# The ConvFFN of a decoder step: the down-projection taken out of the token blocks and made a stage of its own in seven products

## The chip, the cores and the metric

The kernel runs on one core of one Trainium2 chip. The metric is the device time in microseconds of one execution, as the median of several runs. The engines are TensorE (PE in the rows, its weight loads PEld), VectorE (DVE), ScalarE (ACT), GpSimd (POOL) and SyncE (SP), whose queue issues the transfers between DRAM and the on-chip memory SBUF. Products accumulate in PSUM, which has eight banks of 512 float32 columns.

## The reference, cut to what matters

The whole program is one layer of a hybrid decoder for 2048 prompt tokens and 64 sample tokens (8 sequences of 8). The change is in its last part, the ConvFFN:

```python
hf = rmsnorm(x, w['norm_ffn'])
uf = hf @ w['f_wup']                                   # 1024 -> 2 x 2816
fa, fg = uf[..., :D_FF], uf[..., D_FF:]
f_ext = jnp.concatenate([f_buf.astype(fa.dtype), fa], axis=1)
fa_c = causal_dwconv(f_ext, w['f_conv_w'], w['f_conv_b'])   # 3 taps along the tokens
x = x + (jax.nn.gelu(fa_c) * fg) @ w['f_wdown']        # 2816 -> 1024
...
y = rmsnorm(x, norm_final)
```

The matrices are float32. Each factor is held as a high and a low part in `float32r`, and a product of a 128-row piece is three matmuls (`mm3`: high by high, high by low, low by high). Making the two parts of a tile is a "split": ACT casts the tile to its high part, and DVE or POOL subtracts that from the tile for the low part.

## The kernel before, in words

Everything before the ConvFFN (mLSTM, conv module, attention) is the same in both kernels. It leaves the tokens' rows in DRAM (`x2_d`). The ConvFFN then goes over four blocks of tokens, `C_BLOCKS`: three of 512 prompt tokens and one of 512 prompt tokens and the 64 sample tokens.

**Up-projection.** `block_input` reads a block's rows, normalises and transposes them, and writes seven sums of quarters `R[0]` to `R[6]` (for B11, B21, B22, T3, T1, T2, T4; the tokens are cut in two halves and the 1024 features in two halves). `load_pair` does the same on the weight side for two neighbouring tiles of 128 hidden features: it loads 1 MB of `f_wup`, adds and subtracts its quarters (`left_sums`, in the first block only; the later blocks read the sums back from DRAM, `sum_d`) and splits the seven factors into tiles `wt`. `seven_products` then makes two 128-feature tiles for both token halves with seven products in place of eight: each is 4 pieces by 3 matmuls, 12 matmuls with a half block's tokens as columns (256, and 288 in the last block). DVE joins the products from PSUM (`u`, `fe`). Two hidden tiles take one pair for `fa` and one for `fg`, that is 2 x 84 matmuls; between them the taps and the GELU are run (`y`), and after them `y` is multiplied by the second pair's results and split into `ht`.

**Down-projection.** After a group of 4 hidden tiles (`UP_GROUPS`; one group has 2), `load_down` loads and splits their `f_wdown` rows and multiplies `ht` by them: for each tile of 128 tokens and each half of the 1024 output columns, 3 matmuls of 512 columns per hidden tile. The results are added from PSUM to the residual rows `yt`. In program order a group's down-projection stands between the two pairs of the next group (`pend_down`), and the one of the last group of a block stands around `block_input` of the next block. After the last group the rows are normalised with `norm_final` and stored.

**Order.** The order in which each engine's instructions stand is made by a scheduler when the program is built, from data dependences and from the tiles that are free; each engine then runs its own list in order and waits on semaphores. All transfers are in SP's list; a transfer that waits for a tile to come free holds up those behind it. R has one buffer for each of its seven tiles, so the next block's `R[q]` can be written only when the last product that reads the old one is done. The raw weight tiles (`raw`, 4 KB a partition) have six buffers (`RAW_BUFS`), the split ones twelve.

Of the kernel before, what the change touches and what calls it, by code (L numbers as in the profile page):

```python
# [9 lines left out]
F32 = mybir.dt.float32  # L10
# [64 lines left out]
WT_BUFS = (7, 5)  # L75
XT_BUFS = 3
# [4 lines left out]
DOWN_SET = 4  # L81
U_BUFS = 6
UP_GROUPS = [4, 4, 4, 4, 2, 4]

C_BLOCKS = [(0, 0), (4, 0), (8, 0), (12, 1)]
BT = 4
HC = BT * P // 2
HS = S // 2
LO_POOL = (3, 5), (3, 5)
RAW_BUFS = 6  # L90
E_SUM = lambda nc: [nc.vector] * 4
MUL_POOL = (0, 1)


@with_exitstack
def trunk_kernel(ctx: ExitStack, tc: tile.TileContext, i: dict, o: list):
# [1341 lines left out]
    def rows_in(blk, own=(), junk=None):  # L1438

        t0, smp = blk  # L1440
        halves = []
        for z in range(2):
            xts = []
            for tid, r0, nt in [(t0 + 2 * z, 0, P), (t0 + 2 * z + 1, 0, P)] + ([(NT, z * HS, HS)] if smp else []):
                if nt < P or z in own:
                    t = fe_.tile([P, D], F32, name="xt", tag="xt", bufs=XT_BUFS)
                else:
                    t = xw.tile([P, D], F32, name="xt", tag="xt")
# [202 lines left out]
    ahead = rows_in(C_BLOCKS[0], (), junk_rows)  # L1651
# [3 lines left out]
    fe_ = ctx.enter_context(tc.tile_pool(name="fe", bufs=1, reuse_waits="tile"))  # L1655
    wtps = [ctx.enter_context(tc.tile_pool(name="wtf0", bufs=WT_BUFS[0], side="right", reuse_waits="tile"))]
    f2 = ctx.enter_context(tc.tile_pool(name="f2", bufs=2, side="right", reuse_waits="tile"))

    def utile(n):
        return fe_.tile([P, HC + HS], F32, name="u", tag="u", bufs=U_BUFS)[:, :n]  # L1660

    def block_input(blk, rows=None):

        t0, smp = blk
        n = HC + (HS if smp else 0)
        R = [fe_.tile([P, 2, KT // 2, HC + HS], F32R, name=f"R{q}", tag=f"R{q}") for q in range(7)]

# [8 lines left out]
        xts, xts1 = rows or rows_in(blk, (1,))  # L1676
        b11 = [fe_.tile([P, HC + HS], F32, name="b", tag="b", bufs=KT // 2)[:, :n] for _ in range(KT // 2)]

# [33 lines left out]
    def sample_state():  # L1712
        fsr = i["state_ffn_conv"][0].rearrange("b j c -> (b j) c")
        for q0 in range(0, FT, 8):
            nq = min(8, FT - q0)
            t = fe_.tile([P, D], F32, name="xt", tag="xt", bufs=XT_BUFS)
# [50 lines left out]
    def conv_states(q0, nq):  # L1767

        for src, dst, nr in ((carry, fconv_p[0, 0], 2), (cy_s, fconv_s[0].rearrange("b j c -> (b j) c"), 2 * NB)):
# [3 lines left out]
            t = f2.tile([P, BT * P + S], F32, name="fo", tag="y")  # L1773
# [6 lines left out]
    def parts(smp):  # L1780
        return ((slice(0, HC), 0), (slice(HC, HC + HS), 1)) if smp else ((slice(0, HC), 0),)

    for bi, (t0, smp) in enumerate(C_BLOCKS):
        R, n = nxt_.pop()
        npr = BT * P
        ntok = npr + (S if smp else 0)
        tiles = [(t0 + j, P) for j in range(BT)] + ([(NT, S)] if smp else [])
        ys = []
        for tid, nt in tiles:
            yt = xw.tile([P, D], F32, name="yt", tag="xt")  # L1790
            SY.dma_start(yt[:nt], x2_d[tid])
            ys.append(yt)
        if smp:
            sample_state()
        pend_down = []

        def load_down(fbase, gsz, hts, last_):

            wds = []
            for f0 in range(fbase, fbase + gsz, 2):  # L1800
                for z in range(2):
                    raw = raw_tile()
# [131 lines left out]
```

## Time and profile before

| | |
|---|---|
| time, median of 3 runs | 2969.03 us (2966.44 to 2973.68) |
| the profiled execution | 2968.27 us, span 2966.6 us |
| PE busy over the span | 2807.9 us (95%), 17924 matmuls |
| DVE, ACT, POOL busy | 2142.2 us (72%), 1534.5 us (52%), 1109.8 us (37%) |
| moved by DMA | 471.80 MB, 159 GB/s on average |
| ConvFFN | from 1452 us to the end at 2966.6 us |

Busy time is the union of an engine's instructions. A matmul's own duration in the rows is longer than its share of the stream, because matmuls follow each other in a pipeline; what one costs is read from the distance between starts. The chain of work that ended last is 72% PE and 14% DVE over the span.

### The profile page before, as it was taken

To read this page: it belongs to the slowest core of one execution; us is meant where nothing else is said; L and a number is where in the kernel's file an instruction comes from. 1 tells how busy PE (TensorE), PEld (TensorE's weight loads), DVE (VectorE), ACT (ScalarE), POOL (GpSimd) and SP (SyncE) were. 2 spreads that over 40 slices of the span, in tenths; PEclk is the share of its full clock that TensorE was granted. 3 is DMA by queue.
4 is the path that set the end of the run, shared out by engine and by line. 5 is a ranking of instruction groups with operands and counts; after the bars stand their busy time and mean duration, and the time that the engine had idled before them with its cause. 6 is when DMAs were issued, how large, how long until landed. Compare 5 with 4: busy or idle time off the path is not lost.

```text
span 2966.6 us, 49315 instructions
## 1 busy us (share of the span) xinstructions
PE 2807.9 (95%) x17924; PEld 2479.4 (84%) x17924; DVE 2142.2 (72%) x3937; ACT 1534.5 (52%) x3134; POOL 1109.8 (37%) x1299
## 2 busy tenths in 40 slices
PE   7999989999799799899899999999999999999998
PEld 6889889976678688676588988999989999899987
DVE  4588898873123888744598889878797767877776
ACT  4667678871232765412464446655466545544433
POOL 1558565451120632633433325333253222522222
PEclk9999999997899999999899999999999999999999
DMA  7644433244456423656745555655465545644432
GB/s 185 194 139 160 124 97 117 90 161 152 165 184 222 141 82 109 212 193 240 266 162 169 166 171 195 189 160 160 144 219 160 158 135 162 187 131 133 131 116 76
DMA packets 336939, 471.80 MB, mean 159 GB/s; under 512 B 33421, under 2 KB 238707, under 8 KB 336688
## 3 DMA queue, kind: packets, MB, share of 16 engines
q1 hardware_dynamic: 336696, 468.66, 49.2%
q8 instruction: 141, 2.31, 0.3%
q14 instruction: 102, 0.84, 0.1%
HBM read 361.68 MB, written 107.26 MB: 158 GB/s over the span
## 4 chain that ended last, share of the span: by engine, by line
PE 72%; DVE 14%; DMA 6%; issue 4%; ACT 2%; POOL 1%; SPq 1%; DVEq 0%; POOLq 0%; ACTq 0%
PE psA L150 21%; PE psD L150 14%; PE psF L150 14%; PE psE L150 9%; PE psG L150 9%; DVE psG L124 2%; DMA raw<-in_f_wup 2%; DVE wt L127 2%; PE psC L147 1%; PE psB L147 1%; DVE raw L127 1%; DVE acc L124 1%; DVE u L127 1%; DVE wf L127 1%; DMA xt<-x 1%
## 5 line engine op out<-in xcount | busy, mean ns | idle before, releaser
L296 ACT CAST wt<-raw 128x512 fp32r<-128x512 f32 x872 | 528.8, 620 | 529.2 <-PE psA L150 150.6
L127 DVE TENSOR_TENSOR wt<-raw,wt 128x512 fp32r<-128x512 f32 x660 | 512.2, 792 | 123.5 <-ACT wt L296 119.7
L127 POOL TENSOR_TENSOR wt<-raw,wt 128x512 fp32r<-128x512 f32 x212 | 306.5, 1449 | 703.9 <-ACT wt L296 572.2
L150 PE MATMUL psA<-R,wt 128*128 128x256 f32 (+1 forms) x2448 | 334.1, 287 | 4.1 <-DVE R L124 1.6
L150 PEld LDWEIGHTS psA<-R,wt 128*128 128x128 f32 x2448 | 313.8, 190 | 7.7 <-DVE R L124 1.8
L127 POOL TENSOR_TENSOR cside<-cside,cprod 128x512 f32<-128x512 f32 (+2 forms) x248 | 250.9, 1012 | 123.1 <-ACT cprod L119 90.0
L124 DVE SCALAR_TENSOR_TENSOR psG<-ue,vc,psG 128x512 f32<-128x512 f32 (+2 forms) x448 | 256.9, 573 | 22.8 <-ACT psG L119 16.0
L150 PE MATMUL psA<-wt,ht 128*128 128x512 f32 (+1 forms) x768 | 191.0, 395 | 0.0
L150 PE MATMUL psD<-R,wt 128*128 128x256 f32 (+1 forms) x1248 | 178.5, 288 | 6.7 <-DVE R L127 2.8
L150 PE MATMUL psF<-R,wt 128*128 128x256 f32 (+1 forms) x1248 | 179.3, 288 | 4.4 <-DVE R L124 1.7
L150 PE MATMUL psE<-R,wt 128*128 128x256 f32 (+1 forms) x1224 | 174.3, 287 | 5.8 <-DVE R L127 3.0
L150 PE MATMUL psG<-R,wt 128*128 128x256 f32 (+1 forms) x1224 | 175.3, 288 | 1.9 <-DVE R L124 1.3
L150 PEld LDWEIGHTS psD<-R,wt 128*128 128x128 f32 x1248 | 163.7, 191 | 10.4 <-DVE R L127 3.8
L150 PEld LDWEIGHTS psA<-wt,ht 128*128 128x128 f32 (+1 forms) x768 | 140.6, 185 | 34.9 <-DVE u L127 0.2
L150 PEld LDWEIGHTS psF<-R,wt 128*128 128x128 f32 x1248 | 163.4, 190 | 6.2 <-DVE u L127 2.6
L150 PEld LDWEIGHTS psE<-R,wt 128*128 128x128 f32 x1224 | 159.4, 190 | 9.6 <-DVE R L127 4.3
L150 PEld LDWEIGHTS psG<-R,wt 128*128 128x128 f32 x1224 | 160.3, 191 | 3.1 <-DVE R L124 1.6
L119 ACT ACTIVATE cprod<-ue,vc 128x512 f32<-128x512 f32 (+2 forms) x248 | 146.8, 605 | 28.4 <-POOL cside L127 22.0
L150 PE MATMUL psA<-wf,l 128*128 128x512 f32 x516 | 132.2, 404 | 10.8 <-DVE u L127 5.8
L124 DVE SCALAR_TENSOR_TENSOR y<-fe,vc,y 128x512 f32<-128x512 f32 x176 | 130.5, 778 | 14.4 <-ACT y L119 14.4
L127 POOL TENSOR_TENSOR y<-y,u 128x256 f32<-128x256 f32 x110 | 97.8, 898 | 107.0 <-DVE u L127 89.5
L150 PEld LDWEIGHTS psA<-wf,l 128*128 128x128 f32 x516 | 97.8, 193 | 38.7 <-issue 13.2
(608 smaller groups left out, 6096.1 us busy)
## 6 DMA issues: line engine op xcount, KB each, us to landing
raw<-sum SPq DMA_DIRECT2D x132, 512.0 KB
raw<-in_f_wup SPq DMA_DIRECT2D x110, 512.0 KB
raw<-in_f_wdown SPq DMA_DIRECT2D x88, 512.0 KB
xt<-x SPq DMA_DIRECT2D x48, 512.0 KB
sum<-raw SPq DMA_DIRECT2D x44, 512.0 KB
raw<-in_f_wup SPq DMA_DIRECT2D x66, 256.0 KB
xt<-in_x_prompt SPq DMA_DIRECT2D x32, 512.0 KB
x<-xt SPq DMA_DIRECT2D x32, 512.0 KB
```

Of the source, the lines that this page charges most:

```text
L119: A.activation(out, in_, func, bias=bias, scale=scale)
L124: V.scalar_tensor_tensor(out=out, in0=in0, scalar=s, in1=in1, op0=op0, op1=op1)
L127: (eng or V).tensor_tensor(out=out, in0=a, in1=b, op=op)
L147: T.transpose(out, in_, ident[:n, :n])
L150: T.matmul(out, lhsT, rhs, start=start, stop=stop)
L296: A.copy(hi, src)
```

## The change

The down-projection leaves the token blocks. The up-projection is run first for all tokens, in three blocks of 768, 640 and 640 prompt tokens (the last with the 64 sample tokens), so that a matmul has 384, 320 and 352 columns. For each pair of hidden tiles the gated product `y` is not split but summed: its quarters (token half by hidden tile) are combined by `left_sums` into the seven left factors of a product of the same kind, and these go to DRAM (`l_d`; the sample tokens' `y` to `ys_d`). Then a new stage makes the down-projection of the 2048 prompt tokens with seven products in place of eight, factor by factor: for each factor q, `right_factor` loads, adds and splits the eleven 128-row pieces of `f_wdown`'s quarter sums (`w`, 15 buffers), and for each of eight token groups j `left_factor` reads 128 token columns of all eleven pieces from `l_d` (`lr`, 2 buffers) and splits them (`l`, 3 buffers); 33 matmuls of 512 columns follow, and DVE or POOL adds the result to the residual rows `acc`, which stay in SBUF. The sample tokens are multiplied as before, with 132 matmuls. Two of the seven right factors are also written to DRAM and read again (`t2_d`, `t3_d`).

The raw tiles have 4 buffers instead of 6 in the up-projection, the split weights 10 instead of 12, and one of the four sums of the first block goes to POOL.

```diff
-WT_BUFS = (7, 5)
+WT_BUFS = (7, 3)
-UP_GROUPS = [4, 4, 4, 4, 2, 4]
-C_BLOCKS = [(0, 0), (4, 0), (8, 0), (12, 1)]
+C_BLOCKS = [(0, 6, 0), (6, 5, 0), (11, 5, 1)]
-RAW_BUFS = 6
-E_SUM = lambda nc: [nc.vector] * 4
+RAW_BUFS = 4
+E_SUM = lambda nc: [nc.vector, nc.vector, nc.gpsimd, nc.vector]
+DW_BUFS = 15
+E_LEFT = lambda nc: [nc.gpsimd, nc.vector, nc.vector, nc.gpsimd]
...
-                for y in yts:
-                    ht = f3.tile([P, 2, BT * P + S], F32R, name="ht", tag="ht")
-                    split(ht[:, 0, :ntok], ht[:, 1, :ntok], y[:, :ntok])
+            ls = f2.tile([P, 4, HM], F32, name="ls", tag="ls", bufs=1)[:, :, :hc]
+            (a11, a21), (a12, a22) = [[y[:, z, :hc] for z in range(2)] for y in ys]
+            left_sums(ls[:, 2], ls[:, 3], ls[:, 1], ls[:, 0], a11, a12, a21, a22, E_LEFT(nc))
+            SY.dma_start(l_d[bi][0, :, p], a11)
+            SY.dma_start(l_d[bi][1, :, p], a12)
+            SY.dma_start(l_d[bi][6, :, p], a22)
+            SY.dma_start(l_d[bi][2:6, :, p].rearrange("q p t -> p q t"), ls)
...
+            if bi + 1 < len(C_BLOCKS):
+                if p == FP - 3:
+                    rows_next = rows_in(C_BLOCKS[bi + 1])
+                if p == FP - 1:
+                    nxt_.append(block_input(C_BLOCKS[bi + 1], rows_next))
...
+    def right_factor(q, k):
...
+        elif q == T2:
+            t3, b, x = quarter(1, 1, k), quarter(0, 1, k), quarter(0, 0, k)
+            tt(t3, t3, b, ALU.subtract)
+            SY.dma_start(t3_d[k], t3)
+            tt(x, x, t3, ALU.add)
+            SY.dma_start(t2_d[k], x)
+        elif q == T3:
+            x = raw_w(t3_d[k])
...
+        w = dp.tile([P, 2, 512], F32R, name="w", tag="w", bufs=DW_BUFS)
+        split(w[:, 0], w[:, 1], x)
+        return w
+    def left_factor(q, j):
+        raw = dp.tile([P, FP, P], F32, name="lr", tag="lr", bufs=2)
+        r = 0
+        for b, c, m in segments(j):
+            SY.dma_start(raw[:, :, r:r + m], l_d[b][q, :, :, c:c + m])
+            r += m
+        w = dp.tile([P, 2, FP, P], F32R, name="l", tag="l", bufs=3)
+        split(w[:, 0], w[:, 1], raw)
+        return w
...
+    for qi, q in enumerate((B11, B21, T2, T3, T1, B22, T4)):
+        ws = [right_factor(q, k) for k in range(FP)]
...
+        for j in range(NJ):
+            l = left_factor(q, j)
+            if qi == 0 and j == 0:
+                accs = [[acc_rows(z, j) for j in range(NJ)] for z in range(2)]
+            pt = dps()
+            for k in range(FP):
+                mm3(pt, (l[:, 0, k], l[:, 1, k]), (ws[k][:, 0], ws[k][:, 1]), k == 0, k == FP - 1)
...
+            elif q == B22:
+                tt(x01, x01, pt, ALU.add)
+                out_rows_norm(0, j)
             else:
-                pend_down.append(down)
+                tt(x10, x10, pt, ALU.add)
+                out_rows_norm(1, j)
```

Three places show what the order of instructions becomes. The first is PE's list where one token block ends and the next begins (`R` with the larger number is the next block's, `wt,ht` is the down-projection, L147 the transposes of the next block's rows). Before, at the end of the second block:

```order
L150 MATMUL psF<-R_19466,wt 128x256 x12
L150 MATMUL psE<-R_19467,wt 128x256 x12
L150 MATMUL psA<-wt,ht 128x512 x6
L147 MATMUL psB<-ident,xt 128x128 x2
L147 MATMUL psC<-ident,xt 128x128 x2
L150 MATMUL psF<-wt,ht 128x512 x6
L150 MATMUL psG<-wt,ht 128x512 x6
```

And now, at the end of the first block, on the same engine (`R_18897` to `R_18899` are the next block's first three factors):

```order
L150 MATMUL psG<-R_15306,wt 128x384 x12
L150 MATMUL psD<-R_15307,wt 128x384 x12
L147 MATMUL psB<-ident,xt 128x128 x2
L147 MATMUL psB<-ident,xt 128x64
L147 MATMUL psC<-ident,xt 128x128 x2
L147 MATMUL psC<-ident,xt 128x64
L150 MATMUL psF<-R_18897,wt 128x320 x12
L150 MATMUL psE<-R_18898,wt 128x320 x7
L147 MATMUL psB<-ident,xt 128x64
L147 MATMUL psB<-ident,xt 128x128 x2
L150 MATMUL psE<-R_18898,wt 128x320 x3
```

Before, 96 matmuls of the last group's down-projection stand among the transposes; now only the next block's own products stand there.

The second place is SP's list at the end of the last block. Before, in the last block, weight loads of both projections alternate (L1744, L1749 and L1759 load `f_wup` pieces and their sums, L1775 stores the conv state, L1803 loads `f_wdown`):

```order
L1744 DMA raw<-in_f_wup 128x8x128
L1749 DMA raw<-in_f_wup 128x4x128
L1759 DMA raw<-sum_0_19275 128x1024
L1759 DMA raw<-sum_1_19276 128x1024
L1803 DMA raw<-in_f_wdown 128x1024 x4
```

Now the stage's first loads stand behind the last store of left factors (L1860; L1919 loads `f_wdown` pieces, L1958 left factors, L1911 residual rows):

```order
L1858 DMA l_15489<-y 128x320
L1863 DMA ys<-y 128x2x32
L1860 DMA l_15489<-ls 128x4x320
L1919 DMA raw<-in_f_wdown 128x512 x6
L1958 DMA lr<-l_15487 128x11x128
L1919 DMA raw<-in_f_wdown 128x512
L1911 DMA acc<-x_11_197 64x1024
L1919 DMA raw<-in_f_wdown 128x512 x2
L1911 DMA acc<-x_12_198 64x1024
```

Fifteen more loads of residual rows (L1911) or `f_wdown` pieces follow before the second left factor's load.

The third place is SP's list at the third product of the new stage, T2, which has no counterpart before (L1939 and L1941 store the two factors `t3` and `t2`, here of pieces 0 to 2):

```order
L1958 DMA lr<-l_15487 128x11x128 x3
L1958 DMA lr<-l_15488 128x11x128 x2
L1919 DMA raw<-in_f_wdown 128x512 x7
L1939 DMA t_0_26187<-raw 128x512
L1919 DMA raw<-in_f_wdown 128x512
L1941 DMA t_0_26176<-raw 128x512
L1939 DMA t_1_26188<-raw 128x512
L1919 DMA raw<-in_f_wdown 128x512 x2
L1941 DMA t_1_26177<-raw 128x512
```

Three loads and two stores of 256 KB alternate for each of the eleven pieces, with the loads of T2's first five left factors ahead of them; the `raw` tiles here (2 KB a partition) have six buffers. On PE the first three token groups of T2 stand interleaved, piece by piece.

## Rows read from the trace of the kernel before

**Rows 1.** Busy time by stretch: us, PE, PEld, DVE, ACT, POOL, PEclk, DMA share, GB/s.

```profile
1520.00:1840.00 320.00, 311.19 (x2088) 283.12 (x2087) 278.59 (x492) 156.01 (x281) 99.53 (x108) 1.00 0.49 159
1840.00:2190.00 350.00, 347.42 (x2414) 322.48 (x2413) 283.10 (x486) 192.62 (x344) 123.56 (x136) 1.00 0.54 169
```

**Rows 2.** PE's timeline in the second block: start us, us, what.

```profile
1912.77 2.92 PE L150 MATMUL psD<-wt,ht 128*128 128x512 f32 x12
1915.53 2.94 PE L150 MATMUL psF<-wt,ht 128*128 128x512 f32 x12
1918.31 1.59 PE L150 MATMUL psE<-R,wt 128*128 128x256 f32 x12
1919.74 3.02 PE L150 MATMUL psA<-R,wt 128*128 128x256 f32 x24
```

**Rows 3.** PE's timeline in the last block, 288 columns.

```profile
2733.62 3.36 PE L150 MATMUL psA<-R,wt 128*128 128x288 f32 x24
2736.82 0.70 PE L150 MATMUL psE<-R,wt 128*128 128x288 f32 x4
```

**Rows 4.** ACT's timeline: the first tap of the first, second and third block.

```profile
1495.63 1.51 ACT L119 ACTIVATE y<-fe,vc 128x512 f32<-128x512 f32 x2
...
1859.23 1.52 ACT L119 ACTIVATE y<-fe,vc 128x512 f32<-128x512 f32 x2
...
2209.24 1.52 ACT L119 ACTIVATE y<-fe,vc 128x512 f32<-128x512 f32 x2
```

**Rows 5.** DVE's groups by form in the ConvFFN: xcount | busy, mean ns.

```profile
L127 DVE TENSOR_TENSOR wt<-raw,wt 128x512 fp32r<-128x512 f32 x616 | 478.4, 794 | 62.4 <-ACT wt L296 58.9
L124 DVE SCALAR_TENSOR_TENSOR y<-fe,vc,y 128x512 f32<-128x512 f32 x176 | 130.5, 778 | 14.4 <-ACT y L119 14.4
L127 DVE TENSOR_TENSOR raw<-raw 128x512 f32<-128x512 f32 x88 | 64.7, 755 | 13.6 <-DMA raw<-in_f_wup 13.5
L127 DVE TENSOR_TENSOR u<-u,psA 128x256 f32<-128x256 f32 x110 | 44.6, 414 | 3.6 <-PE psA L150 1.9 <-ACT u L1067 0.6
L127 DVE TENSOR_TENSOR y<-y,u 128x256 f32<-128x256 f32 x88 | 38.5, 462 | 0.0
L127 DVE TENSOR_TENSOR u<-u,psA 128x288 f32<-128x288 f32 x38 | 16.7, 450 | 1.9 <-PE psA L150 1.4
L124 DVE SCALAR_TENSOR_TENSOR y<-fs,vc,y 128x64 f32<-128x64 f32 x44 | 15.0, 378 | 0.0
```

**Rows 6.** POOL's and ACT's groups by form in the ConvFFN.

```profile
L127 POOL TENSOR_TENSOR wt<-raw,wt 128x512 fp32r<-128x512 f32 x176 | 257.2, 1464 | 613.6 <-ACT wt L296 496.4 <-issue 52.8 <-DVE fe L127 40.1
L127 POOL TENSOR_TENSOR y<-y,u 128x256 f32<-128x256 f32 x88 | 85.1, 968 | 107.0 <-DVE u L127 89.5 <-ACT y L119 15.9 <-DVE y L124 1.3
L296 ACT CAST wt<-raw 128x512 fp32r<-128x512 f32 x792 | 480.7, 620 | 456.6 <-PE psA L150 149.8 <-PE psD L150 91.0 <-PE psE L150 77.3
```

**Rows 7.** Tile `raw`, second block: duration ns min/median/max, first and last start.

```profile
L127 DVE TENSOR_TENSOR wt<-raw,wt x149: 675/691/1671, 1849.8 to 2188.2; 128x512 fp32r<-128x512 f32 x149
```

**Rows 8.** Tile `R`, 1800 to 1890 us: the second block's factors being written.

```profile
L127 DVE TENSOR_TENSOR R<-u,R x12: 409/637/1175, 1824.0 to 1856.1; 128x256 fp32r<-128x256 f32 x12
L124 DVE SCALAR_TENSOR_TENSOR R<-psC,vc,R x6: 469/476/484, 1814.4 to 1849.0; 128x256 fp32r<-128x256 f32 x6
```

**Rows 9.** Busy time at the start of the ConvFFN, columns as in Rows 1.

```profile
1457.00:1462.00 5.00, 3.06 (x16) 2.66 (x16) 4.66 (x7) 3.93 (x9) 2.96 (x2) 0.80 1.11 338
1462.00:1467.00 5.00, 3.50 (x15) 2.72 (x15) 4.25 (x6) 1.66 (x4) 1.95 (x2) 0.54 1.02 414
1467.00:1472.00 5.00, 2.79 (x8) 1.94 (x9) 5.00 (x9) 4.14 (x9) 3.71 (x4) 0.50 1.03 398
1472.00:1477.00 5.00, 3.19 (x15) 2.77 (x14) 4.86 (x8) 1.91 (x6) 3.58 (x3) 0.50 0.86 268
```

**Rows 10.** PE's timeline at the same place; in brackets the idle time before.

```profile
1452.39 0.69 PE L147 MATMUL psB<-ident,xt 128*128 128x128 f32 x2 [4.08 <-ACT b L119]
...
1455.07 2.93 PE L150 MATMUL psA<-R,wt 128*128 128x256 f32 x12 [0.22 <-ACT R L119]
```

More of the change, by code (lines that the diff above doesn't have):

```diff
@@ L74 @@
 LOW = -3e38
-WT_BUFS = (7, 5)
-XT_BUFS = 3
+WT_BUFS = (7, 3)
 E_B = lambda nc: nc.vector
@@ L1436, in out_rows, with pieces, rows_in @@
             SY.dma_start(x2_d[t], xt)
-    def rows_in(blk, own=(), junk=None):
-        t0, smp = blk
+    def pieces(blk, z):
+        t0, nt, smp = blk
+        hc = nt * P // 2
+        r, end, out = t0 * P + z * hc, t0 * P + (z + 1) * hc, []
+        while r < end:
+            m = min(end, (r // P + 1) * P) - r
+            out.append((r // P, r % P, m))
+            r += m
+        return out + ([(NT, z * HS, HS)] if smp else [])
+    def rows_in(blk, junk=None):
         halves = []
@@ L1443, in rows_in @@
             xts = []
[L1444 to L1448, printed above, removed]
+            for tid, r0, nt in pieces(blk, z):
+                t = xw.tile([P, D], F32, name="xt", tag="xt")
                 SY.dma_start(t[:nt], x2_d[tid][r0:r0 + nt])
@@ L1650, in trunk_kernel @@
             pass
-    ahead = rows_in(C_BLOCKS[0], (), junk_rows)
+    ahead = rows_in(C_BLOCKS[0], junk_rows)
     aps.close()
@@ L1674, in feature @@
             return pt[:, :n]
-        xts, xts1 = rows or rows_in(blk, (1,))
-        b11 = [fe_.tile([P, HC + HS], F32, name="b", tag="b", bufs=KT // 2)[:, :n] for _ in range(KT // 2)]
+        xts, xts1 = rows
+        b11 = [fe_.tile([P, HM], F32, name="b", tag="b", bufs=KT // 2)[:, :n] for _ in range(KT // 2)]
         def put(q, k, x, eng=None, gain=None):
@@ L1778, in trunk_kernel @@
     wdn = i["f_wdown"][0]
-    def parts(smp):
-        return ((slice(0, HC), 0), (slice(HC, HC + HS), 1)) if smp else ((slice(0, HC), 0),)
-    for bi, (t0, smp) in enumerate(C_BLOCKS):
+    l_d = [dram(f"l{b}", [7, P, FP, nt * P // 2]) for b, (_, nt, _) in enumerate(C_BLOCKS)]
+    ys_d = dram("ys", [P, FT, S])
+    for bi, (t0, nt_, smp) in enumerate(C_BLOCKS):
         R, n = nxt_.pop()
[L1785 to L1792, printed above, removed]
+        hc = nt_ * P // 2
+        npr = nt_ * P
@@ new lines, in trunk_kernel, with segments @@
+    us.close()
+    dp = ctx.enter_context(tc.tile_pool(name="dp", bufs=1, reuse_waits="tile"))
+    dps = banks("A", "B", "C", "A", "D", "E", "F", "G")
+    NJ = L // 2 // P
+    starts = [0]
+    for _, nt_, _ in C_BLOCKS:
+        starts.append(starts[-1] + nt_ * P // 2)
+    def segments(j):
+        out, c = [], j * P
+        while c < (j + 1) * P:
+            b = max(b for b in range(len(C_BLOCKS)) if starts[b] <= c)
+            m = min((j + 1) * P, starts[b + 1]) - c
+            out.append((b, c - starts[b], m))
+            c += m
+        return out
@@ new lines, in token_rows, with acc_rows @@
+    def token_rows(z, j):
+        out, r = [], 0
+        for b, c, m in segments(j):
+            t0, nt_, _ = C_BLOCKS[b]
+            out.append((t0 * P + z * (nt_ * P // 2) + c, m, r))
+            r += m
+        return out
+    def acc_rows(z, j):
+        if z == 0 and j < 6:
+            t = xw.tile([P, D], F32, name="acc", tag="xt")
+        else:
+            t = dp.tile([P, D], F32, name="acc", tag=f"acc{z}_{j}")
+        for t0, m, r in token_rows(z, j):
+            while m:
+                k = min(m, P - t0 % P)
+                SY.dma_start(t[r:r + k], x2_d[t0 // P][t0 % P:t0 % P + k])
+                t0, m, r = t0 + k, m - k, r + k
+        return t
```

261 lines of the change are left out of this document (148 added, 113 removed).

## The prediction

> **What bounds the kernel now.** I read the busy time by stretch first. In the ConvFFN PE is busy in 347 of 350 us of the second block, DVE in 283 (81%); in the first block PE is at 97% and DVE at 87% [rows 1]. So I read PE's timeline for what one matmul costs in the stream, as the distance between starts: at 512 columns (1918.31 - 1912.77) / 24 = 231 ns, at 256 columns (1919.74 - 1918.31) / 12 = 119 ns [rows 2], at 288 columns (2736.82 - 2733.62) / 24 = 133 ns [rows 3]. The three lie on a line of 0.437 ns a column with some 7 ns a matmul on top; I read 175 ns at 384, 147 at 320 and 161 at 352 from it.
>
> A block of 512 tokens has 22 x 84 matmuls at 119 ns and 528 at 231 ns, 341 us, and 32 transposes, some 4 us. ACT's first tap stands 363.6 us after the one before it in the first block and 350.0 us in the second [rows 4]. The second block thus loses about 5 us, all that its change of block costs; the first loses 13.6 us more, and it is the one whose DVE also makes weight sums. PE's stream is the bound, and DVE at some 87% begins to hold it up. What the change takes from PE counts fully, and so does every place where it leaves PE without work.
>
> **The matmuls.** The up-projection's three blocks have the same columns in all, in 5544 matmuls instead of 7392: before 5544 x 119.2 + 1848 x 133.3 ns = 907 us, after 1848 x (175 + 147 + 161) = 893: -14 us. The down-projection of the prompt tokens goes from 2112 to 1848 matmuls of 512 columns: 264 x 231 ns = -61 us. The 132 for the sample tokens stay. Together **-75 us**. The Trainium skill ("TensorE: Matmul & The Clock Gate", section "Back-to-back issue gap") puts an isolated matmul at its columns over 2.4 GHz plus 2.5 ns. By that the sum here would be 1848 x 2.5 + 264 x 216 ns = -62 us; the rows stand above it at every width, so they decide.
>
> **The change of block, now uncovered.** Before, 96 matmuls of down-projection (22 us) stand on PE while DVE, ACT and POOL write the next `R`. Now PE has only the next block's own products. From the last product on, DVE's list has to reach the last `R`: four times two operations of 0.48, one of 0.48, three lower halves of 0.4 to 0.7 and a sum of some 0.6 us [rows 8], 3.9 us each at 256 columns and 4.4 at 320 by the slope of the joins [rows 5], so 18 us; among them stand the last pair's products and sums and two weight splits, 5 us. PE has 84 matmuls and 24 transposes for these 23 us, 15 us. It loses 9 us with the last matmuls, twice, against 5 us three times before: **+3 us**. Below, nothing is lost at all (-15). Above, the writing takes as long as now, 1814 to 1857 us [rows 8], 42 us less 15, twice: +39. I take the sum, since nothing else is queued on DVE there.
>
> **The start.** The first block has six tiles to normalise and R is half as wide again (DVE 17 to 23 us), but the two pairs that PE has beside it are longer by 2 x 84 x 56 ns = 9 us. I take nothing.
>
> **Inside the up-projection.** PE now needs 168 matmuls for two hidden tiles with no down-projection between. DVE needs, by busy time over count [rows 5], in the first block 10 splits at 0.78, 6 sums at 0.74, 14 joins at 0.54, 2 products at 0.58, 4 taps at 1.05 and 2 left sums at 0.58, 26.4 us of PE's 29.4 (90%); in the second 20.0 of 24.7 (81%); in the third, with small pieces for the sample tokens, 24.6 of 27.1 (91%). Two blocks stand where one stood at 87%. If each loses what that one lost, **+14 us** net. Below: none loses (-14); above stands the rival on the shared port.
>
> **Between the stages.** The new stage's first load stands behind the last store of left sums on SP. From the last product U, DVE has about six operations of 0.5 us and POOL one of 1.3 us: first load at U+5. Ahead of the first left factor's end lie its store (0.66 MB), six raw pieces (1.57 MB) and itself (0.72 MB); at 340 GB/s, a little under the mean of the four stretches of [rows 9], in which the DMA was full or nearly so, that is 9 us; its split of 1408 columns, 2.75 times the 512 one on ACT and DVE [rows 6, 7], takes 3.6. PE stands still from U to U+18. An idle time of 4 us now leaves the clock at half, and 12 matmuls take 2.93 us instead of 1.43 [rows 9, 10]; one product of 33 at half speed throughout would add 7.6 us, I take 3. The first product ends at U+28.6. Then the second left factor is late: ahead of it are 5.2 MB of residual rows and 1.3 MB of raw pieces, with itself 7.3 MB, 21 us behind the first, and a split: U+39, another 10 us. In all **+31 us**; at 414 GB/s, the best of the four stretches, 26; at 268, the worst, 39.
>
> **T2.** Each of its eleven pieces is three loads and two stores of 256 KB; of six raw tiles three hold a piece, and a load waits for the store before it. They cannot begin before B12's pieces leave the raw tiles, some 5 us after the last product E of B21. 14.4 MB at 340 GB/s is 42 us; with a split and the last matmuls T2's first three groups are done at E+52. PE has the sample parts (66 matmuls, 15 us) and three products (23 us), interleaved piece by piece, to E+38: **+14 us** (6 at 414, 25 at 268 GB/s). T1 and T4 load two pieces each ahead: **+2** (0 to 6). The other factors load one piece of 256 KB in 7.6 us / 11 of PE's time each, and DVE has about 5 of every 7.6 us to do there: nothing.
>
> **The sum:** -75 + 3 + 14 + 31 + 14 + 2 = -11 us. The profiled execution takes 2968.3 us, 0.8 below the median of the runs shown, so I forecast **2958 us**.
>
> **The rivals.**
> - *The forecast*, each wait near my value: 2938 to 2978 us, chance 0.42.
> - *The waits are hidden.* For it: the interleaved order of T2, and that a group's DVE work was hidden under PE in the second block. Against: nothing of PE's is left at the three places. With the lower bounds, -75 - 15 - 14 + 26 + 6 = -72, 2896; half the way to my sum is 2927. Range 2900 to 2938, chance 0.26.
> - *DVE and POOL shut each other out in the up-projection; slower.* DVE's split takes 691 ns at the median and 1671 at most [rows 7], mean 794 [rows 5]: it waits for something that is not in its own list. If DVE operations with both inputs in SBUF and POOL operations exclude each other, two hidden tiles of the first block need 17.2 us of DVE (splits, sums, taps, products) and 14.3 of POOL (four splits and two sums at 1.46, four products and sums at some 1.4 [rows 6]), 31.5 us against PE's 29.4; now it is 20.5 + 7.8 = 28.3 in the 33 us that a pair of tiles takes. If that can be filled wholly, the first block loses 23 us; if only to today's 86%, all three lose 145. The middle, 84, in place of my 28 gives 3014, the range 2978 to 3060. It decides from 20 us above my term. Against: the second block today is at 74% by this count and loses nothing, which says nothing on 90%. Chance 0.17. The Trainium skill has such a rule ("SBUF — State Buffer", section "Who interferes with whom"): a DVE instruction with two SBUF inputs contends with a GpSimd instruction that reads SBUF, and the later one fully blocks. The spread of the splits agrees with it.
> - *The DMA is slower than 340 GB/s in the new stage*: left factors come in rows of 512 bytes, stores and loads alternate. At 268 GB/s the last three terms are 39 + 25 + 6 in place of 47: 2981; lower still, or with PE's clock down longer, up to 3010. Chance 0.13.
> - A change that does not do what it says is excluded by the order: the matmuls are gone. 0.02 is left for the rest.
>
> **How the numbers follow.** About 0.3%, 9 us, is what a measurement can tell from no change. Of the forecast's 0.42, 0.22 lies below 2960, 0.17 within 0.3% and 0.03 above. Faster: 0.22 + 0.26 and half of the rest, 0.49; same 0.17; slower 0.03 + 0.17 + 0.13 and the rest, 0.34. The range 2908 to 3010 leaves out the end of the hidden case and most of the upper half of the port's, together under 0.2.
>
> **What would show it.** In the profile after: PE's starts 175, 147 and 161 ns apart in the three blocks; the first taps of the blocks some 350 us, then 285 apart; two changes of block with about 9 us of lost PE time; PE idle for some 18 us between the last `R` product and the first `w` product, with a load as releaser and the clock at half behind it, and idle again for 10 us before the second; DVE above 85% in the first and third block; T2's first 99 matmuls in some 37 us instead of 23. The prediction is wrong if PE's share in the up-projection falls under 95% (the port), if the gap between the stages is above 45 us or below 20, or if the third product is as dense as the others.

## The result, and the profile after

The changed kernel takes **3001.3 us** (2998.8 to 3003.7, four runs) against 2968.8 for the kernel before in the same session: ratio 1.0113, 95% interval 1.0098 to 1.0129. It is 1.1% slower. I forecast 2958 and faster at 0.49; the time lies in the range (2908 to 3010), on the other side of no change.

The page's first lines for the changed kernel, which answer to the table of before: PE's busy time falls by 40 us with 2096 matmuls and transposes less, and its share of the span falls from 95% to 92%.

```profile
span 2997.0 us, 44306 instructions
PE 2767.7 (92%) x15828; PEld 2436.1 (81%) x15828; DVE 2058.6 (69%) x3432; ACT 1407.6 (47%) x2795; POOL 1165.5 (39%) x1269
```

ACT's timeline, first and last tap of each of the three blocks (answers to [rows 4]):

```profile
1505.43 1.02 ACT L119 ACTIVATE y<-fe,vc 128x768 f32<-128x768 f32 x1
1822.33 1.95 ACT L119 ACTIVATE y<-fe,vc 128x768 f32<-128x768 f32 x2
1873.65 0.92 ACT L119 ACTIVATE y<-fe,vc 128x640 f32<-128x640 f32 x1
2121.09 1.74 ACT L119 ACTIVATE y<-fe,vc 128x640 f32<-128x640 f32 x2
2185.87 0.93 ACT L119 ACTIVATE y<-fe,vc 128x640 f32<-128x640 f32 x1 [0.54 <-DVE fe L127]
2457.80 1.74 ACT L119 ACTIVATE y<-fe,vc 128x640 f32<-128x640 f32 x2 [5.21 <-DVE fe L127]
```

A block's ten inner pairs of hidden tiles lie between its first and last tap, a change of block between the last tap of one and the first of the next. Busy time of these stretches and of three in the new stage, columns as in [rows 1]:

```profile
1505.40:1822.30 316.90, 295.96 (x1664) 290.20 (x1663) 284.60 (x377) 124.06 (x201) 157.82 (x139) 0.99 0.53 176
1822.30:1873.70 51.40, 45.11 (x209) 37.48 (x208) 42.01 (x69) 38.32 (x74) 30.91 (x37) 0.77 0.45 140
1873.70:2121.10 247.40, 247.40 (x1688) 247.17 (x1688) 214.48 (x323) 120.09 (x204) 115.57 (x121) 1.00 0.62 198
2121.10:2185.90 64.80, 57.20 (x245) 45.95 (x245) 43.21 (x74) 31.88 (x62) 30.07 (x33) 0.63 0.43 129
2185.90:2457.80 271.90, 271.53 (x1705) 270.07 (x1704) 245.19 (x451) 132.18 (x237) 136.97 (x160) 1.00 0.57 175
2470.00:2488.10 18.10, 0.68 (x7) 0.27 (x4) 7.76 (x16) 5.13 (x8) 3.21 (x3) 0.64 0.76 226
2488.10:2524.20 36.10, 20.09 (x67) 14.98 (x68) 11.55 (x13) 8.74 (x12) 0.00 (x0) 0.71 1.08 298
2651.70:2700.90 49.20, 32.68 (x104) 21.53 (x102) 26.11 (x37) 10.99 (x16) 4.07 (x3) 0.85 0.90 293
```

The second and third block run dense. Time goes in the first block, in both changes of block, before and behind the stage's first product (sixth and seventh row), and in T2 (last row). PE's timeline gives the price of a matmul at 384, 320, 352 and 512 columns, and the idle time ahead of the places where it stands (in brackets): the start, the second change (two rows), and the first two products of the stage.

```profile
1459.29 0.90 PE L147 MATMUL psB<-ident,xt 128*128 128x128 f32 x3 [14.62 <-ACT b L119]
...
1804.06 2.24 PE L150 MATMUL psG<-R,wt 128*128 128x384 f32 x12
1806.14 2.24 PE L150 MATMUL psA<-R,wt 128*128 128x384 f32 x12
...
1900.04 1.92 PE L150 MATMUL psG<-R,wt 128*128 128x320 f32 x12
1901.81 1.33 PE L150 MATMUL psF<-R,wt 128*128 128x320 f32 x8
...
2134.72 1.22 PE L147 MATMUL psB<-ident,xt 128*128 128x128 f32 x4 [2.63 <-ACT b L119]
2150.62 0.47 PE L147 MATMUL psB<-ident,xt 128*128 128x128 f32 x1 [4.03 <-ACT xt L119]
...
2301.88 2.08 PE L150 MATMUL psF<-R,wt 128*128 128x352 f32 x12
2303.80 2.08 PE L150 MATMUL psE<-R,wt 128*128 128x352 f32 x12
...
2488.10 1.22 PE L150 MATMUL psA<-w,l 128*128 128x512 f32 x2 [17.43 <-ACT l L296]
2513.28 1.22 PE L150 MATMUL psB<-w,l 128*128 128x512 f32 x2 [15.13 <-ACT l L296]
2524.19 7.64 PE L150 MATMUL psC<-w,l 128*128 128x512 f32 x33
2531.67 7.64 PE L150 MATMUL psA<-w,l 128*128 128x512 f32 x33
```

A matmul costs 2.08 / 12 = 173 ns at 384 columns, 1.77 / 12 = 147 at 320, 1.92 / 12 = 160 at 352 and 7.48 / 33 = 227 at 512. In the following table a stretch's loss is its length less its matmuls at these prices (before: at those of the prediction, 342.1 us for a block). Before, the third change of block has to be read too, which I had not done: the first tap of the last block in ACT's timeline of the kernel before stands 361.1 us after that of [rows 4]'s last row, 17.8 us over its matmuls.

```profile
2570.30 1.53 ACT L119 ACTIVATE y<-fe,vc 128x512 f32<-128x512 f32 x2 [0.98 <-DVE fe L127]
```

The prediction counted DVE's list from the old block's last product to the last operation on the next `R`, 23 us. In the changed kernel these last operations stand on DVE's timeline at the two changes as follows; the last products of the old blocks had ended at 1833.3 and 2129.4 us, so it took 35 and 54 us.

```profile
1867.92 0.49 DVE L127 TENSOR_TENSOR R<-u,R 128x320 fp32r<-128x320 f32 x1
2183.39 0.52 DVE L127 TENSOR_TENSOR R<-u,R 128x352 fp32r<-128x352 f32 x1
```

| term | forecast | measured | how |
|---|---|---|---|
| matmuls | -75 | -88 | 1848 x (173 + 147 + 160) ns + 1980 x 227 ns = 888 + 449, against 907 + 518 |
| start | 0 | +9 | end of the last attention product to first tap 61.8 us, before 47.8; 4.5 of the difference are longer matmuls |
| inside the up-projection | +14 | +15 | 25.7 + 0 + 3 us, before 13.6 |
| changes of block | +3 | +30 | (51.3 - 26.9) + (64.8 - 25.8) = 63.4, before 7.9 + 7.9 + 17.8 = 33.6, transposes (3 to 4 us each) in both |
| between the stages | +31 | +39 | 17.4 idle, then 66 matmuls (15.0 us) in 36.1 |
| T2 | +14 | +26 | 103 matmuls (23.3 us) in 49.2 |
| T1, T4 | +2 | +1 | PE waits once, 1.4 us, in T1 (at 2810.7 us) |
| sum | -11 | +32 | from the end of the last attention product to the end 1553.3 us, before 1518.7: +35; 3 us are not assigned |

### The profile page after: what moved, and what is told of

Read it like the earlier page. It is cut to its first block, busy times and chain, and to the rows that moved or that the text cites. A ratio compares the mean times of both kernels' runs of the same rounds, so it can differ in the third digit from the quotient of the medians.

```text
span 2997.0 us, 44306 instructions
## 1 busy us (share of the span) xinstructions
PE 2767.7 (92%) x15828; PEld 2436.1 (81%) x15828; DVE 2058.6 (69%) x3432; ACT 1407.6 (47%) x2795; POOL 1165.5 (39%) x1269
## 5 line engine op out<-in xcount | busy, mean ns | idle before, releaser
L296 ACT CAST wt<-raw 128x512 fp32r<-128x512 f32 x542 | 328.3, 618 | 450.7 <-DMA raw<-sum 79.7
L127 DVE TENSOR_TENSOR wt<-raw,wt 128x512 fp32r<-128x512 f32 x374 | 317.4, 858 | 90.2 <-ACT wt L296 85.6
L150 PE MATMUL psA<-R,wt 128*128 128x384 f32 (+2 forms) x1848 | 335.0, 328 | 11.3 <-DVE u L127 5.4
L150 PE MATMUL psD<-R,wt 128*128 128x384 f32 (+2 forms) x924 | 173.3, 330 | 8.4 <-ACT R L296 2.9
L150 PE MATMUL psG<-R,wt 128*128 128x384 f32 (+2 forms) x924 | 172.8, 329 | 7.2 <-DVE u L127 6.3
L150 PE MATMUL psF<-R,wt 128*128 128x320 f32 (+2 forms) x924 | 171.2, 329 | 4.9 <-DVE u L127 4.3
L150 PE MATMUL psE<-R,wt 128*128 128x320 f32 (+2 forms) x924 | 171.6, 328 | 3.3 <-DVE u L127 2.8
L119 ACT ACTIVATE cprod<-ue,vc 128x512 f32<-128x512 f32 (+2 forms) x248 | 146.8, 605 | 28.7 <-POOL cside L127 21.4
L124 DVE SCALAR_TENSOR_TENSOR y<-fe,vc,y 128x640 f32<-128x640 f32 (+1 forms) x132 | 133.6, 1046 | 30.8 <-ACT y L119 30.8
L150 PE MATMUL psA<-w,l 128*128 128x512 f32 x462 | 116.2, 401 | 33.8 <-ACT l L296 17.4
L150 PE MATMUL psA<-wf,l 128*128 128x512 f32 x516 | 132.4, 404 | 12.6 <-DVE u L127 5.8
L150 PEld LDWEIGHTS psA<-w,l 128*128 128x128 f32 x462 | 87.9, 192 | 58.7 <-ACT w L296 19.1
```

The source lines that it names most:

```text
L119: A.activation(out, in_, func, bias=bias, scale=scale)
L124: V.scalar_tensor_tensor(out=out, in0=in0, scalar=s, in1=in1, op0=op0, op1=op1)
L127: (eng or V).tensor_tensor(out=out, in0=a, in1=b, op=op)
L150: T.matmul(out, lhsT, rhs, start=start, stop=stop)
L296: A.copy(hi, src)
```

## The experiments

The theory after this reading: the saved matmuls are real, and each piece of the loss has its own cause, DVE's list and late rows at the changes of block, the order of transfers in the new stage, the engines DVE and POOL in the first block. Rivals: the half clock causes the loss at the changes (granted clock 0.77 and 0.63 there); the new stage is short of bandwidth in any order. Times are given by the ratio to the kernel before; the changed kernel stands at 1.0113.

**1. Blocks of 6, 6 and 4 row tiles** instead of 6, 5 and 5.

```diff
-C_BLOCKS = [(0, 6, 0), (6, 5, 0), (11, 5, 1)]
+C_BLOCKS = [(0, 6, 0), (6, 6, 0), (12, 4, 1)]
```

> The blocks are cut as 6, 6 and 4 row tiles with the sample tokens, in place of 6, 5 and 5: no 64-row pieces, six row tiles in each block for the six row buffers, and the same columns in all (384 + 384 + 288 = 384 + 320 + 352). Changed kernel: 3001.3 us; its second change of block loses some 39 us of matmul time, its first some 23. Theory A, late rows: at the second change the last two of eight row tiles wait for a buffer, are normalised after the change has begun, and ACT's list stands behind them. Then the second change falls to 23 us or less, the first a little too (4 normalisations instead of the odd pieces), the total to 2975 to 2988. Theory B, DVE's list of joins, splits and R's halves sets the length: the work is the same, both changes stay, 2997 to 3005. Theory C, the clock at half does: as B, unless the pauses that lower it go with the rows.

Measured: 1.0066 (1.0045 to 1.0087), 14 us less. The second change falls from 64.8 to 45.1 us (taps at 2172.02 and 2217.13), the first stays (52.7). What the edit takes away, the late rows and the 64-row pieces together, was worth some 20 us in the second change and next to nothing in the first. The second block, now as wide as the first but without weight sums, takes 29.1 us a pair where the first takes 31.8: width is not what slows the first.

**2. Residual rows loaded where they are added to.**

```diff
-            if qi == 0 and j == 0:
-                accs = [[acc_rows(z, j) for j in range(NJ)] for z in range(2)]
+            if qi < 2:
+                accs[qi].append(acc_rows(qi, j))
```

> The residual rows of the new stage are loaded where they are first added to (first half at the first product, second half at the second), so that the second left factor follows the first on the queue. Changed kernel: PE stands 17.4 us before the first product of the stage and 15.1 us before the second. Theory A, the 5.2 MB of rows ahead of the second left factor make the second pause: it falls to about 4 us (0.72 MB and a split), the first stays at 17, and the total falls by 8 to 14 us, to 2987 to 2993. Rival, the transfers of the first 50 us are too many in any order: the pause moves to the third or a later group or to the second factor, total within 3 us of 3001.

Measured: 1.0080 (1.0062 to 1.0098), 10 us less; the interval touches the changed kernel's at its end. The wait of 15.1 us before the second product is gone; part comes back later, 1.6 us before the third and 6.4 before the fifth (`psD`), as PE's timeline of this run shows:

```profile
2488.85 1.22 PE L150 MATMUL psA<-w,l 128*128 128x512 f32 x2 [17.14 <-ACT l L296]
2508.41 0.73 PE L150 MATMUL psC<-w,l 128*128 128x512 f32 x2 [1.61 <-ACT l L296]
2533.62 1.22 PE L150 MATMUL psD<-w,l 128*128 128x512 f32 x2 [6.40 <-ACT l L296]
```

**3. T2 without its stores.**

```diff
-            SY.dma_start(t3_d[k], t3)
             tt(x, x, t3, ALU.add)
-            SY.dma_start(t2_d[k], x)
...
-            x = raw_w(t3_d[k])
+            x, b = quarter(1, 1, k), quarter(0, 1, k)
+            tt(x, x, b, ALU.subtract)
```

(T4 likewise, from four pieces.)

> T3 and T4 are made anew from the pieces of the down-projection's weights (two and four loads a piece), and T2 stores nothing. Changed kernel: T2's first three groups (99 matmuls, 22.4 us of work) take some 44 to 48 us. Theory A, the stores hold the raw tiles and so T2's loads: they fall to 28 to 36 us, and T4, with four loads a piece, loses part of it; total 2983 to 2997. Rival, T2 is bound by its three loads and the splits of its first left factors, not by the stores: T2 stays above 42 us and T4 adds 5 to 10: 3003 to 3012.

Measured: 1.0097 (1.0076 to 1.0118); by time alone it can't be told from the changed kernel. In the trace the eleven pieces of T2 take 32.3 us (2658.0 to 2690.3) in place of 45.8 (2651.7 to 2697.5), and T4 gets a new pause of 3.6 us. So the stores held T2, by some 13 us; in the changed kernel SP's list waits in this stretch most for them:

```profile
SPq L1919 <- DMA t<-raw: 15.1, 15, 2.0
```

**4. All weight sums of the first block on DVE.**

```diff
-E_SUM = lambda nc: [nc.vector, nc.vector, nc.gpsimd, nc.vector]
+E_SUM = lambda nc: [nc.vector] * 4
```

> In the first block all four weight sums go to DVE, none to POOL. Changed kernel: 31.7 us for two hidden tiles in the first block, PE's own time 29.4, DVE busy 90%, POOL 50%. Theory A, DVE's list is the bound there: two sums of 0.7 us more for each pair of hidden tiles, the first block 10 to 16 us longer, total 3011 to 3017. Theory B, DVE and POOL keep each other out: DVE gets 1.5 us, POOL loses 2.9, so the first block is 5 to 15 us shorter: 2986 to 2996. Theory C, neither, the loads queued behind the stores of the sums: within 3 us of 3001.

Measured: 1.0044 (1.0028 to 1.0060), 20 us less: theory B, and more than it gave (2986 to 2996; the median is 2978.8). DVE gets two sums more for each pair of hidden tiles, and the first block's ten pairs take 302.0 us (taps at 1495.89 and 1797.92) instead of 316.9, 15 us less. DVE's groups there, first in the changed kernel, then in this run (split, sum, and a join that reads PSUM):

```profile
L127 DVE TENSOR_TENSOR wt<-raw,wt 128x512 fp32r<-128x512 f32 x100 | 93.7, 941 | 3.5 <-ACT wt L296 3.5
L127 DVE TENSOR_TENSOR raw<-raw 128x512 f32<-128x512 f32 x57 | 51.1, 897 | 18.1 <-DMA raw<-in_f_wup 9.0 <-POOL wt L127 8.4 <-DVE wt L127 0.2
L127 DVE TENSOR_TENSOR u<-u,psA 128x384 f32<-128x384 f32 x34 | 18.3, 545 | 0.2
```

```profile
L127 DVE TENSOR_TENSOR wt<-raw,wt 128x512 fp32r<-128x512 f32 x101 | 83.0, 828 | 1.0 <-ACT wt L296 1.0
L127 DVE TENSOR_TENSOR raw<-raw 128x512 f32<-128x512 f32 x76 | 56.3, 762 | 11.4 <-DMA raw<-in_f_wup 6.1 <-POOL wt L127 5.1
L127 DVE TENSOR_TENSOR u<-u,psA 128x384 f32<-128x384 f32 x34 | 18.3, 545 | 0.1
```

19 more sums cost 5 us, since each operation with two SBUF inputs became shorter (split 941 to 828 ns, sum 897 to 762). The join from PSUM keeps its 545.

**5. The four edits together.**

> The four edits together (6, 6 and 4 row tiles; residual rows late; no stores in T2; all weight sums on DVE). Against before they stood at 1.0066, 1.0080, 1.0097 and 1.0044, the changed kernel at 1.0113: apart they gave 14, 10, 5 and 20 us. Theory A, the losses lie at different places and add: 3001 - 49 = 2952, ratio 0.990 to 0.999. Rival, part of each gain was time that another wait takes over (or the length of the queue of the next one): half of the sum, 2977, ratio 1.001 to 1.006.

Measured: **2950.1 us, 0.9946 (0.9928 to 0.9965)**: faster than both kernels, and than the one before by 0.5%. The gains add: 50 us by the ratios, 49 apart. It is the reference of the runs below. Its changes of block still take 55.8 and 45.3 us.

**6. PE kept busy at the changes of block.**

```diff
+WARM = 3
...
             pt = tps()
...
+            for _ in range(WARM if blk[0] else 0):
+                mm(pt[:, :P], ident, ident)
             for t, nt in xts:
                 transpose(pt[:, c:c + nt], t[:nt, k * P:(k + 1) * P])
```

> As the four edits together, and at the two changes of block three extra 128 x 128 float32 products of the identity stand ahead of each of the 16 groups of transposes, in the same bank, overwritten by them; they use no data of the kernel. They show what PE's half clock costs at a change. Theory C, the half clock is a cost of its own: with PE busier the granted clock stays higher, and each change shrinks by 4 to 8 us, total 8 to 16 us below the kernel without them. Theory B, DVE's list sets the change: the products fill time in which PE would wait, each change as long as without them or up to 10 us longer.

**7. Sixteen lower halves left out at each change.**

```diff
+    SHORT = (T1, T2, T3, T4)
...
-            split(R[q][:, 0, k, :n], R[q][:, 1, k, :n], x, gain, eng)
+            if blk[0] and q in SHORT:
+                A.copy(R[q][:, 0, k, :n], x)
+            else:
+                split(R[q][:, 0, k, :n], R[q][:, 1, k, :n], x, gain, eng)
...
```

> As the four edits together, but the lower halves of the factors T1, T2, T3 and T4 are left out in the second and third block (the matmuls stay, and take the upper half in its place), so the results are not the reference's. It takes 16 operations of some 0.48 us, about 8 us, off DVE in each change and nothing off ACT and PE. Theory B, DVE's list sets the change of block: each change 5 to 8 us shorter, total 10 to 16 us below the kernel with all of them. Rival, ACT's order (casts behind the normalisation of late rows) or the half clock sets it: changes within 2 us of those without this edit, total within 5.

Measured: run 6 0.9970 (0.9947 to 0.9992), not to be told from run 5; run 7 0.9914 (0.9890 to 0.9937), 9 us less than run 5 by the ratios, with intervals that overlap at their ends. Busy time of the two changes of block, in runs 5, 6 and 7 in this order:

```profile
1803.90:1859.70 55.80, 45.55 (x218) 39.66 (x218) 42.58 (x69) 40.51 (x77) 35.35 (x35) 0.85 0.40 131
2151.00:2196.30 45.30, 42.27 (x244) 37.15 (x244) 42.04 (x71) 25.05 (x54) 26.84 (x30) 0.89 0.55 180
```

```profile
1799.50:1855.80 56.30, 50.89 (x301) 47.67 (x300) 45.63 (x70) 40.58 (x77) 35.94 (x36) 0.91 0.40 131
2146.50:2193.50 47.00, 46.22 (x321) 42.42 (x320) 42.23 (x71) 25.68 (x54) 27.41 (x31) 1.00 0.51 168
```

```profile
1809.60:1856.90 47.30, 41.47 (x217) 37.54 (x216) 34.99 (x57) 38.48 (x75) 28.76 (x32) 0.89 0.49 159
2148.30:2187.40 39.10, 37.41 (x236) 32.68 (x236) 32.86 (x59) 25.04 (x53) 21.24 (x26) 1.00 0.57 188
```

In run 6 the granted clock is 0.91 and 1.00 instead of 0.85 and 0.89, and the changes are no shorter (+0.5 and +1.7 us). That alone does not clear the clock, since the products take PE's time themselves, 10.9 and 8.3 us by the distances of their starts. The chain of work in the second change says more: at the full clock it runs mostly over DVE, and over the extra products (`psB` and `psC` of L151; the lines of this run's kernel are numbered one higher) for only 6.7% of the 47.0 us, 3.1 us. Without them that change could not be shorter than 43.9 us, against 45.3 in run 5, so the half clock cost little there, by this estimate at most 1.4 us.

```profile
by line: DVE wt L128 17.2%; DVE R L128 16.0%; DVE u L128 14.6%; issue 8.3%; DVE y L125 7.9%; ACT y L120 4.0%; PE psB L151 3.9%; PE psD L151 3.8%; PE psB L148 3.7%; PE psC L148 3.0%; DVE u L125 2.9%; PE psC L151 2.8%; DVE R L125 2.8%; PE psA
```

For the first change, whose clock stayed at 0.91, run 6 does not decide. In the changed kernel's own second change the half clock did lengthen the loss, by how much no run shows: once the late rows are there, PE is busy without a break and the chain runs over PE but for 0.6 us of ACT.

```profile
2152.60:2185.90 33.30, 33.23 (x131) 27.02 (x132) 23.94 (x42) 14.61 (x32) 19.51 (x21) 0.57 0.43 128
```

In run 7 the changes are 8.5 and 6.2 us shorter: the making of the factors sets their length. But the edit takes less from DVE than the expectation says. T1's four lower halves stand on POOL (`E_T1`), so twelve operations leave DVE and four leave POOL; of run 5's first change these two rows, DVE and POOL, are gone:

```profile
L127 DVE TENSOR_TENSOR R<-u,R 128x384 fp32r<-128x384 f32 x12 | 10.5, 891 | 2.3 <-ACT R L296 2.3
L127 POOL TENSOR_TENSOR R<-u,R 128x384 fp32r<-128x384 f32 x4 | 5.0, 1250 | 0.6 <-ACT R L296 0.6
```

DVE's busy time falls by 7.6 and 9.2 us, POOL's by 6.6 and 5.6. Run 7 does not separate the two, nor what came with the clock, which rose to 0.89 and 1.00.

**8. The first left factor ahead of the right pieces.**

```diff
+        l0 = left_factor(q, 0) if qi == 0 else None
         ws = [right_factor(q, k) for k in range(FP)]
...
-            l = left_factor(q, j)
+            l = left_factor(q, j) if qi or j else l0
```

> As the four edits together, and the first left factor of the new stage is issued ahead of the eleven right pieces. Now six pieces (1.57 MB) stand ahead of it, and PE stands still 17.2 us before the first product. Theory A, the first left factor's end sets the pause: it lands some 4 us sooner and its split runs while the pieces come, the pause is 12 to 14 us, total 3 to 5 below. Rival, the right pieces and their splits set it: the pause stays at 16 to 18.

Measured: 0.9964 (0.9948 to 0.9979), not to be told from run 5 (the intervals overlap). The first pause falls to 12.6 us, as theory A had it, and the gain is lost again at the third product (4.1 us) and behind it: the fifth (`psD`) begins 46.8 us after the first, in run 5 37.2. It is what the rival of run 2 had expected: what is left of this pause moves with the order of the transfers.

**9 and 10. Extra POOL work**, six products or sixteen fills a pair of hidden tiles on a scratch tile `zz`.

```diff
+            if bi == 1:
+                for _ in range(6):
+                    tt(zz, zz, zz, ALU.mult, G)
```

(In run 10: `for _ in range(16): G.memset(zz, 0.0)`.)

> As the four edits together, and in the second block POOL gets six extra products of 512 columns (two inputs in SBUF, a scratch tile that nothing else reads) for each pair of hidden tiles, some 8 us in 29.3. That block loses nothing now: PE 100% busy, DVE 80%, POOL 42%, a DVE split 833 ns in the mean of 675 at least. Theory B, a POOL operation that reads SBUF keeps out DVE operations with two SBUF inputs: DVE's SBUF operations (some 13 us a pair undisturbed) and POOL's (12 + 8 us) no longer fit into 29.3 us; the mean split rises above 950 ns, a pair takes 31 to 35 us, the block 17 to 60 us longer. Rival, the engines run side by side and only the order of results counts: split at 800 to 860 ns, and at most 5 us more in all, from POOL's own work coming later.

> As the run with six extra POOL products, but sixteen fills of the same scratch tile (memset, no input) stand in their place. If DVE is slowed by POOL's reading of SBUF, DVE's splits keep their 833 ns and the block its 29.3 us for a pair, unless the fills take POOL's list beyond its time; if any busy POOL, or only the lateness of its results, does it, the time rises as with the products for the same busy time.

Measured: 1.0118 (1.0099 to 1.0137) with the products, 0.9976 (0.9962 to 0.9991) with the fills. The order placed both in the first block, in its first five pairs, not in the second, since nothing ties them to a block; so the pair of 29.3 us of the expectation is one of 30.7 there. For about the same time of POOL in some 122 us (60.6 and 66.9 us), DVE's groups read as follows, first with products, then with fills:

```profile
L127 DVE TENSOR_TENSOR wt<-raw,wt 128x512 fp32r<-128x512 f32 x32 | 38.1, 1198 | 1.4 <-ACT wt L296 1.4
L127 DVE TENSOR_TENSOR raw<-raw 128x512 f32<-128x512 f32 x24 | 31.3, 1327 | 0.5 <-DMA raw<-in_f_wup 0.2
L127 DVE TENSOR_TENSOR u<-u,psA 128x384 f32<-128x384 f32 x10 | 5.3, 543 | 0.0
L127 POOL TENSOR_TENSOR zz<-zz 128x512 f32<-128x512 f32 x44 | 60.6, 1377 | 1.6
```

```profile
L127 DVE TENSOR_TENSOR wt<-raw,wt 128x512 fp32r<-128x512 f32 x39 | 32.0, 820 | 2.2 <-ACT wt L296 2.1
L127 DVE TENSOR_TENSOR raw<-raw 128x512 f32<-128x512 f32 x32 | 24.0, 771 | 6.3 <-DMA raw<-in_f_wup 3.3 <-POOL wt L127 2.8
L127 DVE TENSOR_TENSOR u<-u,psA 128x384 f32<-128x384 f32 x14 | 7.6, 545 | 0.0
L1828 POOL MEMSET zz<- 128x512 f32 x127 | 66.9, 527 | 5.2
```

A pair takes 40.9 us with the products ((1641.65 - 1519.02) / 3, by the taps), 31.2 with the fills ((1638.40 - 1513.67) / 4). Beside POOL's products, which read SBUF, DVE's splits and sums are 46% and 72% longer than beside its fills, which only write; with the fills (820 and 771 ns) they are no longer than without them (826 and 805 over the same place in run 5), and joins from PSUM are untouched. The Trainium skill ("SBUF — State Buffer", section "Who interferes with whom") says just this: a DVE instruction with two SBUF inputs contends with a GpSimd instruction that reads SBUF, not with one that only writes it. The runs agree.

**11. POOL in place of DVE for eight lower halves** of the next block's factors.

```diff
-E_B = lambda nc: nc.vector
-E_T3 = lambda nc: nc.vector
+E_B = lambda nc: nc.gpsimd
+E_T3 = lambda nc: nc.gpsimd
```

> As the four edits together, but POOL in place of DVE makes the lower halves of B11 and T3 of the next block's factors: 8 of the 28, some 3.8 us off DVE and some 7 us onto POOL in each change of block and at the start. Theory B in its simple form (DVE's list alone sets the change): each change 2 to 4 us shorter, total 4 to 8 us less. If POOL and DVE keep each other out, what DVE gains is lost to POOL's reads: no change within 4 us, or 2 to 8 us longer.

Measured: 0.9980 (0.9963 to 0.9997), 10 us more than run 5. The first change is 1.1 us shorter (54.7), the second 3.4 us longer (48.7), and the start, where the same halves are made, 5.0 us longer (65.2 from the last attention product to the first tap, in run 5 60.2). Work handed to POOL does not relieve DVE as work left out does.

**The ConvFFN alone.** The part ahead of the ConvFFN, which no edit touches, does not take the same time in every execution: in the profiled ones its last attention product ends between 1434.9 us (run 4) and 1452.9 us (run 10). The times above carry such differences. From that point to the end, in one execution of each, the ConvFFN takes:

| kernel | us | kernel | us |
|---|---|---|---|
| before | 1518.7 | run 6 | 1507.7 |
| changed | 1553.3 | run 7 | 1488.6 |
| run 1 | 1536.4 | run 8 | 1507.6 |
| run 2 | 1549.3 | run 9 | 1558.6 |
| run 3 | 1542.9 | run 10 | 1508.2 |
| run 4 | 1530.1 | run 11 | 1516.0 |
| run 5 | 1507.1 | | |

In this count the four edits give 17, 4, 10 and 23 us apart and 46 together, run 7 gives 18.5 more, and runs 6, 8 and 10 are within 1.1 us of run 5.

## Why the prediction was wrong

**The failed step: "The change of block, now uncovered".** It said 9 us with each change, +3 in all; the table has +30, 27 of the 43 us by which the sum is off. Three things were wrong in it. First, it counted 23 us from the old block's last product to the last operation on `R`; it took 35 and 54. The old block's last joins, products and left sums, the new block's weight splits and the new `R` share DVE's list, which is busy for 42 us of the first change. Run 7 shows that the making of the factors, on DVE and POOL together, sets the length in the combined kernel. Second, "nothing else is queued on DVE there" overlooked ACT: the last block has eight pieces of rows for six buffers, so two are loaded and normalised inside the change, and PE works at half clock behind them; run 1 takes that away together with the 64-row pieces, some 20 us. The upper bound (+39) still holds the measured +30. Third, I read one change of before for three; the last one there cost 17.8 us with its transposes where the others cost 7.9, so the error on the changed kernel's own two changes is larger than the 27 show.

**T2**, +26 instead of +14: the mechanism was right (loads wait for the stores ahead of them, run 3), the size not. I counted bytes at 340 GB/s; the stretch moves 293, at which the 14.4 MB take 49 us and not 42. Behind the lower rate, and the some 5 us that are left, may stand the chain of load, sum, store and next load of each piece, since SP's list waits 15.1 us for the stores there; no run tells a slow transfer from such waits.

**The start**, +9 instead of 0. PE is idle for 14.6 us there, where it was 4.1 [rows 10]; what it waits for is ACT, whose list has five casts of weight parts and the work on two later row tiles ahead of `b`, and which itself waits there 3.4 us for a sum on DVE and 1.7 us for a row tile. This was read, not tested; in the combined kernel the pause is still 13.9 us.

**Between the stages**, +39 instead of +31: the first pause was right (17.4 for 18 forecast), the second longer (15.1 for 10), and the 66 matmuls, at a granted clock of 0.71, cost 6 us more (0.9 of it waits for splits) in place of 3. Run 2 shows the residual rows as the cause of the second pause, run 8 that a part of the two only moves.

**Inside the up-projection**, +15 for +14, but that the number came out is luck, since the reason was another. I expected the first and third block to lose for DVE's share of 90%; the third has 90% and loses 3 us. The first block loses 25.7 us, 15 of them because POOL reads SBUF beside DVE: the rival in which DVE and POOL shut each other out is real as a mechanism (runs 4, 9 and 10), but worth the 15 us that run 4 took from the first block, not the 84 us that I gave it. That the time falls into this rival's range (2978 to 3060) is chance: it was to decide from 48 us of loss in the up-projection, and there are 28.7.

**The matmuls** were right, and a little low (-88 for -75): in the new stage a matmul of 512 columns costs 227 ns, not the 231 of [rows 2], over 1980 of them.

**The rival of a slower DMA** got its terms nearly right: 39 + 25 + 6 us at 268 GB/s, measured 39 + 26 + 1. The rows show 298 GB/s between the first two products and 293 in T2, where I had taken 340. The 7.3 MB that I counted ahead of the second product take 24 us at 298 GB/s, and this product starts 25.2 us after the first. So the rate that I chose is the second step that failed: some 12 of the 20 us by which these terms are off, 5 in the second pause and 7 in T2, where the waits for the stores may be what makes the rate.

**The signs.** None of the three by which the prediction was to be wrong came up: PE's share from the first to the last tap of the up-projection is 96.3% (93.4% in the first block), the gap between the stages 39 us, and T2 is not dense. None of them watched the changes of block by themselves.

Two readings were off by little. 1848 matmuls at 119 ns and 528 at 231 are 342 us, not 341, so a change of before lost 4 us beside its transposes, not 5. And the 2.93 us of [rows 10] are a duration, while the 1.43 beside it is a distance of starts; by starts the twelve took 2.72.

## What to carry to other kernels

Work that a change takes off the bounding engine may have been cover: count, for each place that loses it, the whole list of every other in-order engine between the last old and the first new product, not only the new operations, and read each such place of the old profile, not one. Moving work from DVE to POOL was no relief here, where both read SBUF. When a large change loses, its losses can be local: four small edits gave back 50 us here, and the large change was then worth 16 us after all (12 in the ConvFFN alone). Before a filler is taken as proof that a half clock costs nothing, ask how much of the engine's time the filler itself takes, and whether it stands in the chain.

## What the runs showed of the hardware that I had not expected

For about the same busy time, POOL's products and POOL's fills differ widely in what they do to DVE: a split, 675 ns at least [rows 7], takes 1198 ns in the mean beside products and 820 beside fills. A higher granted clock need not shorten a stretch: at the second change of block filler products raised it from 0.89 to 1.00, and the change took 1.7 us longer, its chain mostly on DVE. Where PE itself is the chain the clock has to count: behind the late rows of the changed kernel PE was busy for 33.2 of 33.3 us at a granted clock of 0.57.
